# Second feed-forward product: left factors built on chip, residual and weight sums added by DMA

## Chip, cores and metric

The kernel runs on 1 core of one Trainium2 chip, in fp32 accuracy. The metric is the device time of one execution in microseconds (us).

## What is computed

One encoder layer on 512 tokens of width 2048: a branch of gated linear recurrence (mLSTM) and a branch of differential attention, mixed by gates, then a feed-forward block of width 5632. What the change touches is the end of it:

```
x = x + (g_m * branch_m + g_a * branch_a) @ w_out[l]
h2 = _rmsnorm(x, norm2_w[l])
gate, up = jnp.split(h2 @ w_ffn_in[l], 2, axis=-1)
x = x + (jax.nn.silu(gate) * up) @ w_ffn_out[l]
...
return _rmsnorm(x, final_norm_w)
```

## The kernel before

Every product is made of 128x128 by 128x512 matmuls. To keep fp32 accuracy each factor is split into a high part (a cast on ScalarE, line 151) and a low part (the difference on VectorE, line 152), and three matmuls stand for one (`mm3`).

The earlier products (aqk, av, mv, mqk, mo, ga, gm, ba, bm) are plain. The last three, wo (w_out), fi (w_ffn_in) and fo (w_ffn_out), go through `seven`: a block product of 2 by 2 blocks made with seven products instead of eight. A group g is 512 rows of the inner dimension. For it the weight comes as four blocks, 11, 12, 21 and 22, each a raw tile of 128x1024 fp32 (0.524 MB). Loads a, b, c bring 11, 12, 22, and loads d, e, f bring 21, 12, 22 once more. A chunk has three stages: Q1, Q6, Q5 for every group, then Q2, Q7, Q3 for every group, then Q4 for every group. Each is a *piece*: one split right factor and 12 matmuls. The sums of weights are made on VectorE: T2 = (b + a) + c for Q6 (lines 306 and 308), e + f for Q7 (line 314), T2 + d for Q4 (line 320). Three pairs of PSUM banks (a, b, c) take the results; `post` runs when a stage's last group is done.

wo has 2 chunks of 4 groups, fi 11 (fi0 to fi10) of 4 groups. fo takes its 11 groups in lots of 4, 4 and 3, with 2 chunks for each lot: fo0_0, fo0_1, fo1_0, fo1_1, fo2_0, fo2_1.

The left factors are made by `make_forms`: from the four transposed blocks X11, X12, X21, X22 come seven forms (X11, S1, S2, S3, X12, S4, X22), each split, 14 half tiles of 128x512 fp32 (0.262 MB). For fi they are made from x1 (transposed by `x1_turn`) and stay on chip. For fo, fi's `post` makes them as soon as a chunk is gated (`turned`) and stores all 14 to DRAM on SyncE's queue (line 685); `lot_forms` loads them again, 56 for a lot of four, on ScalarE's queue (line 733), called when Q5 of the chunk before is done.

`added` does the residual: at Q1 it loads eight tiles of the residual (x for wo, x1d for fo) on ScalarE's queue (line 591), adds the results to them on VectorE and GpSimd (lines 593 to 609), and `final` stores them to x1d or, in the last lot, normalizes and writes the output.

The order is the program's, with three helpers. `take` makes pieces two ahead (AHEAD), `load` issues raw loads on SyncE's queue up to two sources past the piece that is made, into 5 raw buffers; `later` puts a step after so many nanoseconds of matmuls. High and low parts have 3 buffers each. The framework adds the semaphores and may order the instructions of an engine by expected readiness.

Of the kernel before, what the change touches and what calls it, by code (L numbers as in the profile page):

```python
# [12 lines left out]
F32 = mybir.dt.float32  # L13
F32R = mybir.dt.float32r
# [102 lines left out]
def build(ctx, tc, a, out):  # L117
# [7 lines left out]
    tpool = ctx.enter_context(tc.tile_pool(name="tpool", bufs=41))  # L125
# [168 lines left out]

    FORMS = ("X11", "S2", "S1", "X12", "S3", "S4", "X22")

    def seven(name, src, ng, forms, post):

        first = len(pieces)

        def raw(g, half, lot, n):
            return source(f"{name}_{n}{g}", src(g, half, lot))

        def t2_make(r11, r12, r22, t2, g):
            def make(nm):
                V.tensor_tensor(raws[r12], raws[r12], raws[r11], ALU.add)
# [20 lines left out]
        t2 = {}  # L327
        for g in range(ng):
            r = [raw(g, 0, 0, "a"), raw(g, 0, 1, "b"), raw(g, 1, 1, "c")]
            piece(f"{name}_q1{g}", r[0], held(lambda r=r: raws[r[0]]))  # L330
            piece(f"{name}_q6{g}", r[2], t2_make(*r, t2, g))
            piece(f"{name}_q5{g}", r[2], held(lambda r=r: raws[r[1]]))
        for g in range(ng):
            r = [raw(g, 1, 0, "d"), raw(g, 0, 1, "e"), raw(g, 1, 1, "f")]
            piece(f"{name}_q2{g}", r[0], t4_make(r[0], t2, g))
            piece(f"{name}_q7{g}", r[2], t3_make(r[1], r[2]))
            piece(f"{name}_q3{g}", r[2], held(lambda r=r: raws[r[2]]))
        for g in range(ng):
# [819 lines left out]
```

## Time and profile before

| | us |
|---|---|
| median of 3 runs | 2817.01 (2814.28 to 2817.61) |
| profiled execution | 2818.14 |
| its span | 2816.4 |
| TensorE busy | 2688.4 (95%) |
| VectorE busy | 1914.6 (68%) |
| ScalarE busy | 1173.3 (42%) |
| GpSimd busy | 206.8 (7%) |
| DMA | 477.03 MB, 169 GB/s on the mean |

The products before w_out fill the span up to 1210.9 us, wo runs to 1391.1, fi to 2297.2, fo to 2803.6. "Granted clock" is the share of TensorE's full clock that was granted in a stretch; "DMA share" is the mean busy share of the core's 16 DMA engines. Matmuls overlap in the pipeline, so the distance from one start to the next is what a matmul costs, and not its own duration.

### The profile page before, as it was taken

How to read it: one execution, taken by the hardware profiler on the slowest of the kernel's cores; microseconds unless marked ns; L12 is line 12 of the kernel's file. 1: busy time of each engine (PE TensorE's matmuls, PEld its weight loads, DVE VectorE, ACT ScalarE, POOL GpSimd, SP SyncE). 2: the span in 40 equal slices, each digit the busy share in tenths (PEclk: the TensorE clock that was granted, in tenths of full speed). 3: DMA queues.
4: the chain of work that ended last, by engine and by line, in shares of the span. 5: the costliest groups of instructions: out<-in, count | busy, mean ns of one | idle time of the engine just before them, and what ended most of it. 6: DMA issues, size and time to landing. Idle time of an engine off the chain costs nothing.

```text
span 2816.4 us, 33558 instructions
## 1 busy us (share of the span) xinstructions
PE 2688.4 (95%) x12736; PEld 2227.1 (79%) x12736; DVE 1914.6 (68%) x2385; ACT 1173.3 (42%) x1659; POOL 206.8 (7%) x208
## 2 busy tenths in 40 slices
PE   8999999999999999989999999999999798789897
PEld 6888888888998888877777788888877677577676
DVE  6677775333444433677988888888888777467677
ACT  5444443222444432334745555544445343233343
POOL 3000000000000000011000000000000001110111
PEclk9999999999999999999999999999999999899999
DMA  6433232333222232455446665655566876867845
GB/s 204 125 93 91 77 109 102 112 112 120 90 85 93 80 110 97 140 170 199 160 157 213 224 209 206 205 191 183 201 215 219 282 258 229 301 237 243 285 167 177
DMA packets 168850, 477.03 MB, mean 169 GB/s; under 512 B 20376, under 2 KB 20936, under 8 KB 168688
## 3 DMA queue, kind: packets, MB, share of 16 engines
q1 hardware_dynamic: 125280, 392.89, 40.8%
q10 hardware_dynamic: 35616, 63.46, 6.8%
q0 software_dynamic: 7792, 18.54, 2.5%
q8 instruction: 100, 1.64, 0.2%
q14 instruction: 62, 0.51, 0.1%
HBM read 402.96 MB, written 61.36 MB: 165 GB/s over the span
## 4 chain that ended last, share of the span: by engine, by line
PE 70%; DVE 12%; DMA 11%; issue 3%; ACT 2%; POOL 1%; ACTq 1%; SPq 0%; DVEq 0%; POOLq 0%
PE fi_b L147 9%; PE ga_b L147 6%; PE gm_b L147 6%; PE aqk_b L147 5%; PE fi_c L147 5%; DVE wlo_fi_q L152 4%; PE fi_a L147 4%; PE fo_b L147 3%; PE mqk_b L147 3%; PE mo_b L147 3%; PE bm_b L147 3%; PE ba_b L147 3%; PE fo_a L147 3%; PE mv_p L147 3%; DMA raw_fi_f<-in_w_ffi 3%
## 5 line engine op out<-in xcount | busy, mean ns | idle before, releaser
L151 ACT CAST whi_fi_q<-fi_q_t 128x1024 fp32r<-128x1024 f32 x88 | 92.5, 1052 | 150.2 <-DVE fi_q_t L308 70.1
L147 PE MATMUL fo_c<-whi_fo_q,fs_S 128*128 128x512 f32 x352 | 119.6, 401 | 13.9 <-ACT whi_fo_q L151 13.4
L147 PE MATMUL fo_a<-whi_fo_q,fs_X 128*128 128x512 f32 x352 | 123.4, 412 | 2.7 <-ACT whi_fo_q L151 2.6
L147 PE MATMUL fo_b<-whi_fo_q,fs_S 128*128 128x512 f32 x352 | 120.0, 401 | 2.1 <-DVE fo_x L593 1.6
L152 DVE TENSOR_TENSOR wlo_fi_q<-fi_q_t,whi_fi_q 128x1024 fp32r<-128x1024 f32 x88 | 106.6, 1221 | 10.2 <-ACT whi_fi_q L151 9.0
L147 PE MATMUL aqk_b<-xh,whi_aqk 128*128 128x512 f32 x256 | 101.3, 398 | 7.7 <-ACT whi_aqk L151 7.7
L147 PE MATMUL aqk_b<-xl,whi_aqk 128*128 128x512 f32 x256 | 101.5, 397 | 3.9 <-DVE xl L483 3.9
L702 POOL TENSOR_TENSOR fv<-fv,fv 128x512 f32<-128x512 f32 x22 | 44.3, 2033 | 794.5 <-ACT fv L701 794.5
L147 PE MATMUL aqk_b<-xh,wlo_aqk 128*128 128x512 f32 x256 | 100.8, 394 | 0.3 <-DVE wlo_aqk L152 0.3
L147 PE MATMUL ga_b<-xh,whi_ga 128*128 128x512 f32 x256 | 99.9, 390 | 0.0
L147 PE MATMUL gm_b<-xh,whi_gm 128*128 128x512 f32 x256 | 99.7, 389 | 0.0
L147 PE MATMUL ga_b<-xl,whi_ga 128*128 128x512 f32 x256 | 99.7, 389 | 0.0
L147 PE MATMUL ga_b<-xh,wlo_ga 128*128 128x512 f32 x256 | 99.7, 389 | 0.0
L147 PE MATMUL gm_b<-xl,whi_gm 128*128 128x512 f32 x256 | 99.6, 389 | 0.0
L147 PE MATMUL gm_b<-xh,wlo_gm 128*128 128x512 f32 x256 | 99.6, 389 | 0.0
L147 PE MATMUL fo_a<-wlo_fo_q,fs_X 128*128 128x512 f32 x176 | 74.4, 423 | 24.9 <-DVE wlo_fo_q L152 24.9
L152 DVE TENSOR_TENSOR wlo_gm<-raw_gm,whi_gm 128x1024 fp32r<-128x1024 f32 x32 | 39.2, 1225 | 84.4 <-ACT whi_gm L151 84.4
L314 DVE TENSOR_TENSOR raw_fi_e<-raw_fi_e,raw_fi_f 128x1024 f32<-128x1024 f32 x44 | 56.0, 1272 | 57.6 <-DMA raw_fi_f<-in_w_ffi 57.6
L147 PEld LDWEIGHTS fo_c<-whi_fo_q,fs_S 128*128 128x128 f32 x352 | 68.6, 195 | 29.4 <-ACT whi_fo_q L151 14.2
L147 PEld LDWEIGHTS fo_a<-whi_fo_q,fs_X 128*128 128x128 f32 x352 | 70.3, 201 | 18.4 <-ACT whi_fo_q L151 3.5
L147 PEld LDWEIGHTS fo_b<-whi_fo_q,fs_S 128*128 128x128 f32 x352 | 68.4, 194 | 18.6 <-DVE fo_x L593 2.8
L147 PE MATMUL fi_c<-whi_fi_q,h_S4h 128*128 128x512 f32 x176 | 69.5, 396 | 13.0 <-ACT whi_fi_q L151 13.0
(494 smaller groups left out, 8500.9 us busy)
## 6 DMA issues: line engine op xcount, KB each, us to landing
raw_fi_a<-in_w_ffi SPq DMA_DIRECT2D x44, 512.0 KB, 4.6
raw_fi_b<-in_w_ffi SPq DMA_DIRECT2D x44, 512.0 KB, 3.5
raw_fi_c<-in_w_ffi SPq DMA_DIRECT2D x44, 512.0 KB, 4.7
raw_fi_d<-in_w_ffi SPq DMA_DIRECT2D x44, 512.0 KB, 4.9
raw_fi_e<-in_w_ffi SPq DMA_DIRECT2D x44, 512.0 KB, 4.5
raw_fi_f<-in_w_ffi SPq DMA_DIRECT2D x44, 512.0 KB, 4.5
fs_S<-fg_S ACTq DMA_DIRECT2D x88, 256.0 KB, 4.7
fs_X<-fg_X ACTq DMA_DIRECT2D x66, 256.0 KB, 4.9
```

What stands on the lines that cost most here:

```text
L147: T.matmul(dst, lhs[l], rhs[r], start=first and i == 0, stop=last and i == 2, skip_group_check=skip)
L151: A.copy(hi, src)
L152: V.tensor_tensor(lo, src, hi.bitcast(F32), ALU.subtract)
L314: V.tensor_tensor(raws[r12], raws[r12], raws[r22], ALU.add)
L702: G.tensor_tensor(v5[i], v5[i], v1[i], ALU.subtract)
```

## The change

- Raw buffers go from 5 to 6, loads run three sources ahead instead of two, and the work tiles go from 41 to 39.
- A source may have a second part (`plus`): GpSimd's queue adds it to the raw tile by an accumulating DMA once the plain load has landed. So b arrives as 11 + 12 and e as 12 + 22, and the sums of lines 306 and 314 are gone. Weight blocks 11 and 22 are read once more for that.
- The pieces go Q1, Q5, Q6, then Q2, Q3, Q7 (the last group Q7, Q3, Q2), then Q4.
- fi keeps only the four transposed blocks of each chunk (`turned`, half a chunk at a time, after Q2 and after Q4), stored on ScalarE's queue. fo loads three of them and then all four on GpSimd's queue (`loaded`) and builds the seven forms again on ScalarE and VectorE, one step behind each piece (`ahead`, `work`), from the start of Q2 in the chunk before. The left factors of h2 are made in the same way, for the first two column blocks by way of DRAM.
- The residual: Q1's result is copied into three tiles by ScalarE, the other results are added by VectorE alone. In fo0 and fo1 the tile is added to x1d by an accumulating DMA; in wo and fo2 the residual is added to the tile by one before the tile's square is taken.
- The last scaling is split: three of the four tiles of a row are multiplied by the norm's weight early, and the last factor goes to ScalarE for two tiles and VectorE for two.

```diff
-            raw = wpool.tile([P, src.shape[-1]], F32, tag="raw", name=f"raw_{name}", bufs=5)
+            raw = wpool.tile([P, src.shape[-1]], F32, tag="raw", name=f"raw_{name}", bufs=6)
             nc.sync.dma_start(raw, src)
+            if plus is not None:
+                G.dma_start(raw, plus, accum_op=ALU.add)
...
-            load(need + 2)
+            load(need + 3)
...
+    def work(must=False):
+        if behind:
+            ready_, fn = behind[0]
+            while must and not ready_():
+                tasks.pop(0)[1]()
+            if ready_():
+                behind.pop(0)
+                fn()
...
-                V.tensor_tensor(raws[r12], raws[r12], raws[r11], ALU.add)
...
-                V.tensor_tensor(raws[r12], raws[r12], raws[r22], ALU.add)
...
+        for g in order:
+            r = [raw(g, 0, 0, "a"), raw(g, 0, 1, "b", (0, 0)), raw(g, 1, 1, "c")]
+            add("Q1", g, r[0], held(lambda r=r: raws[r[0]]))
+            add("Q5", g, r[1], held(lambda r=r: raws[r[1]]))
+            add("Q6", g, r[2], t2_make(r[1], r[2], g))
+        for g in order:
+            if g != order[-1]:
+                r = [raw(g, 1, 0, "d"), raw(g, 1, 1, "f"), raw(g, 0, 1, "e", (1, 1))]
...
+                w = take(it)
+                while LEFT[q_] not in forms(g):
+                    work(True)
...
+                if g == order[-1]:
+                    post(q_, bank)
+                work()
...
+    def loaded(name, g, out, src):
+
+        def load1():
+            out["ld1"] = X = {k: half(f"{name}_1{k}") for k in ("X11", "X21", "X22")}
+            for k, t in X.items():
+                G.dma_start(t, src[k].rearrange("p (k c) -> p k c", k=2))
...
+        def s4():
+            X = out["ld2"]
+            V.tensor_tensor(X["X12"], X["X12"], X["X22"], ALU.subtract)
+            V.tensor_tensor(X["X12"], X["X12"], X["X21"], ALU.subtract)
+            factor(name, g, 10, out, "S4", X["X12"])
...
+        return (load1, [x11, s1, s2]), (load2, [x12, s3, s4, x22])
+
+    def ahead(steps):
+
+        for n, (ld, fns) in enumerate(steps):
+            if n == 0 and ld:
+                ld()
+            nxt = steps[n + 1][0] if n + 1 < len(steps) else None
+
+            def head(fn=fns[0], nxt=nxt):
+                if nxt:
+                    nxt()
+                fn()
+            behind.extend([(lambda: True, fn) for fn in [head] + fns[1:]])
...
+        def fetch(q, i):
+            G.dma_start(x[q, i], src(*place(q, i)), accum_op=ALU.add)
+
+        def end(q, i):
+            t, c = place(q, i)
+            if final:
+                final(t, c, x[q, i])
+            else:
+                G.dma_start(x1d[t][c], x[q, i], accum_op=ALU.add)
...
                 if q_ == "Q1":
...
+                    for q, sc in ((22, -1.0), (12, -1.0), (21, 1.0)):
+                        A.activation(tile_(q, i), a_[i], AF.Copy, scale=sc)
+                    if final:
+                        fetch(21, i)
...
+                elif q_ == "Q7":
+                    V.tensor_tensor(x[22, i], x[22, i], b_[i], ALU.subtract)
+                    if final:
+                        fetch(22, i)
+                    end(22, i)
...
+            if q_ == "Q2":
+                later(5000, lambda: turned(f"fg{j}", u2, 0, X, 0, fgd[j]))
+            elif q_ == "Q4":
+                later(8000, lambda: turned(f"fg{j}", v5, 0, X, 1, fgd[j]))
...
+        both = [loaded(f"fs{g}", i, fgf[g], fgd[g]) for i, g in enumerate(LOTS[m])]
+        ahead([b[0] for b in both] + [b[1] for b in both])
...
+        def final(t, c, x):
+            j = t_(f"x2j{t}_{c}")
+            A.activation(j, x, AF.Square, accum_out=ss3p[:, t * 4 + c:t * 4 + c + 1])
```

## Rows read from the trace of the kernel before

**Rows 1.** The page's line of TensorE: busy us (share of the span) and instructions.
```profile
PE 2688.4 (95%) x12736; PEld 2227.1 (79%) x12736; DVE 1914.6 (68%) x2385; ACT 1173.3 (42%) x1659; POOL 206.8 (7%) x208
```

**Rows 2.** Stretches: bm; then wo0, wo1, fi1, fi10, fo0_0 to fo2_1, the tail.
```profile
core 0: us, PE busy (x) PEld busy (x) DVE busy (x) ACT busy (x) POOL busy (x), PEclk, DMA share, GB/s
1124.00:1211.00 87.00, 87.00 (x386) 72.03 (x385) 62.25 (x96) 29.85 (x40) 6.43 (x12) 1.00 0.42 139
...
1210.90:1297.50 86.60, 79.49 (x337) 64.27 (x336) 69.00 (x74) 37.81 (x49) 9.42 (x6) 0.94 0.57 186
1297.50:1391.10 93.60, 87.36 (x394) 69.69 (x392) 75.51 (x84) 54.10 (x89) 9.46 (x6) 0.96 0.52 175
...
1471.90:1552.30 80.40, 78.67 (x353) 64.39 (x352) 69.68 (x72) 39.92 (x51) 3.00 (x2) 1.00 0.60 205
...
2193.50:2297.20 103.70, 84.67 (x353) 67.19 (x352) 70.11 (x72) 39.70 (x51) 3.12 (x2) 0.90 0.84 297
2297.20:2386.20 89.00, 81.29 (x353) 65.81 (x352) 70.62 (x73) 37.61 (x47) 11.32 (x6) 0.94 0.68 233
2386.20:2492.20 106.00, 86.36 (x338) 67.44 (x337) 59.45 (x56) 30.19 (x30) 9.44 (x6) 0.90 0.85 289
2492.20:2576.30 84.10, 79.54 (x337) 64.69 (x336) 61.67 (x58) 30.48 (x30) 9.44 (x6) 0.96 0.63 211
2576.30:2672.80 96.50, 82.81 (x337) 65.59 (x336) 60.45 (x57) 30.31 (x30) 9.46 (x6) 0.95 0.86 288
2672.80:2739.50 66.70, 61.07 (x253) 49.10 (x253) 47.72 (x46) 26.68 (x35) 9.43 (x6) 0.92 0.53 180
2739.50:2803.60 64.10, 60.26 (x253) 48.01 (x251) 46.73 (x51) 25.91 (x37) 12.86 (x12) 0.97 0.46 154
2803.60:2816.40 12.80, 0.16 (x1) 0.00 (x0) 7.93 (x16) 1.33 (x4) 1.10 (x2) 0.60 0.65 238
```

**Rows 3.** Chain that ended last, bm's matmuls: start us, us, engine, tile, count.
```profile
1124.04 87.04 PE bm_b L147 x384
```

**Rows 4.** Stretch of one transposition in fi, its instructions alone (PE, PEld, ACT).
```profile
1481.20:1484.20 3.00, 2.24 (x16) 1.77 (x16) 1.95 (x7) 1.00 0.59 220
```

**Rows 5.** Timelines of ScalarE and TensorE in fo0_1: start us, us [idle before <-releaser].
```profile
2444.92 1.04 ACT L151 CAST whi_fo_q<-raw_fo_f 128x1024 fp32r<-128x1024 f32 x1 [20.95 <-DMA fs_X<-fg_X]
...
2446.01 1.22 PE L147 MATMUL fo_c<-whi_fo_q,fs_S 128*128 128x512 f32 x2 [9.21 <-ACT whi_fo_q L151]
```

**Rows 6.** The stretch of that gap, columns as in rows 2.
```profile
2430.00:2447.00 17.00, 7.45 (x22) 5.35 (x22) 6.65 (x6) 2.08 (x3) 3.63 (x2) 0.72 0.99 348
```

**Rows 7.** Waits, whole span and wo: us in total, times, longest us.
```profile
SPq L198 <- DVE wlo_fi_q L152: 501.4, 187, 7.2
...
ACT wo_v L586 <- DMA wo_x<-in_x: 12.3, 2, 9.1
```

**Rows 8.** Groups of instructions: busy us, mean ns of one | idle before.
```profile
L152 DVE TENSOR_TENSOR wlo_fi_q<-fi_q_t,whi_fi_q 128x1024 fp32r<-128x1024 f32 x80 | 96.8, 1221 | 8.5 <-ACT whi_fi_q L151 7.2
...
L306 DVE TENSOR_TENSOR raw_fi_b<-raw_fi_b,raw_fi_a 128x1024 f32<-128x1024 f32 x40 | 48.8, 1221 | 37.4 <-DMA raw_fi_b<-in_w_ffi 37.4
...
L152 DVE TENSOR_TENSOR fg_S1l<-fg_S,fg_S1h 128x512 fp32r<-128x512 f32 x9 | 6.2, 683 | 0.0
...
L586 ACT COPY fo_v<-fo_a 128x512 f32<-128x512 f32 x12 | 7.1, 588 | 28.2 <-DMA fo_x<-x1d 16.0 <-PE fo_a L147 4.9 <-issue 4.0
```

**Rows 9.** DMA queues (q1 SyncE's, q0 GpSimd's), and an issue: KB, us to landing.
```profile
q1 hardware_dynamic: 125280, 392.89, 40.8%
...
q0 software_dynamic: 7792, 18.54, 2.5%
...
fo_x<-x1d ACTq DMA_DIRECT2D x48, 256.0 KB, 5.5
```

**Rows 10.** GpSimd's timeline in bm and in fo2_1: DMA issues and additions.
```profile
1161.16 1.07 POOL L524 DMA_DIRECT2D mixa<-mixa_d  x2 [2.53 <-DVE mix_X L530]
...
2765.47 2.31 POOL L596 TENSOR_TENSOR fo_x<-fo_x,fo_v 128x512 f32<-128x512 f32 x1 [1.50 <-DMA fo_x<-x1d]
2767.73 2.23 POOL L771 DMA_DIRECT2D fnw<-in_fnw  x4
2769.97 2.53 POOL L594 TENSOR_TENSOR fo_x<-fo_x,fo_v 128x512 f32<-128x512 f32 x2
```

More of the change, by code (lines that the diff above doesn't have):

```diff
@@ L338, in seven, with add @@
-        for g in range(ng):
-            piece(f"{name}_q4{g}", 0, held(lambda g=g: t2[g]))
+        def add(q_, g, need, make):
+            piece(f"{name}_{q_}{g}", need, make)
+            seq.append((q_, g))
+        for g in order:
[3 more added lines that the diff above has]
+            add("Q6", g, r[2], t2_make(r[1], r[2], g))
@@ L642, in wo_chunk @@
-        inner = added(f"wo{n}", n, lambda t, c: a["x"][t][:, c * 512:(c + 1) * 512], final)
-        def post(q_, bank):
-            inner(q_, bank)
-            if n == 1 and q_ == "Q5":
-                for c in env.pop("turns"):
-                    x1_turn(c)
-        seven(f"wo{n}", lambda g, h_, l: a["w_out"][n, g, h_, l], 4, lambda g: mixf[g], post)
+            A.activation(j, x, AF.Square, accum_out=ss2p[:, t * 4 + c:t * 4 + c + 1])
+            x1[t, c] = x
+            i = t // 2
+            if (2 * i, c) in x1 and (2 * i + 1, c) in x1:
+                pair = [x1.pop((2 * i + k, c)) for k in range(2)]
+                later(4000, lambda: turned(f"h2{c}", pair, 0, h2X[c], i,
+                                           h2d[c] if n == 0 else None,
+                                           lambda kk: n2w[:, c * 4 + kk:c * 4 + kk + 1]))
@@ new lines, in start @@
+        def start(q_):
+            if n == 1 and q_ == "Q2":
+                for g in range(4):
+                    h2f[g] = {}
+                p0, p1 = (loaded(f"h2{c}", c, h2f[c], h2d[c]) for c in range(2))
+                p2, p3 = (kept(f"h2{c}", c, h2f[c], h2X[c]) for c in (2, 3))
+                ahead([p0[0], p1[0], p0[1]])
+                for c, p in ((3, p3), (2, p2)):
+                    when(lambda c=c: len(h2X[c]) >= 4, p[0])
+                when(lambda: True, [p1[1][0]] + p1[1][1])
+                when(lambda: True, p3[1] + p2[1])
@@ L651, in rstd2 @@
+        seven(f"wo{n}", lambda g, h_, l: a["w_out"][n, g, h_, l], range(4), lambda g: mixf[g],
+              added(f"wo{n}", n, lambda t, c: a["x"][t][:, c * 512:(c + 1) * 512], final), start)
     def rstd2():
@@ L756, in norm, with start @@
             pow_rstd(r, ss, D, 1)
[L757 to L766 removed]
+            for k, (c, x) in enumerate(mine):
+                if k == 3:
+                    V.scalar_tensor_tensor(x, x, r, env["fnw"][c], ALU.mult, ALU.mult)
+                elif k == 2:
+                    V.tensor_scalar(x, x, r, None, ALU.mult)
+                else:
+                    A.activation(x, x, AF.Copy, scale=r)
+                (nc.sync if k > 1 else nc.scalar).dma_start(
+                    out[t][:, c * 512:(c + 1) * 512], x)
+        def start(q_):
+            if q_ == "Q2" and n == 1 and not last:
                 lot_forms(m + 1)
[L768 removed]
+            if q_ == "Q1" and n == 0 and last:
                 env["fnw"] = [t_(f"fnw{c}") for c in range(4)]
@@ L773, in fo_chunk @@
         lot = LOTS[m]
[L774 to L775 removed]
+        seven(f"fo{m}_{n}", lambda g, h_, l: a["w_ffo"][n, g, h_, l], lot, lambda g: fgf[g],
+              added(f"fo{m}_{n}", n, *((lambda t, c: x1d[t][c], final) if last else ())), start)
     fin = {}
```

347 lines of the change are left out of this document (167 added, 180 removed).

## Prediction

> **What bounds the kernel now.** I read the page first: TensorE is busy 95% of the span [rows 1], so a gain must come from its gaps. The second view is the table of stretches, one for each chunk of the two last products and w_out [rows 2]. Its first row is a stretch of bm, an ordinary projection: TensorE 87.00 of 87.00 us, with VectorE at 62.25 us (72%) and DMA at 0.42. The chain of waits prices a full matmul there: 384 in 87.04 us, 226.7 ns each [rows 3]. That makes a floor: a chunk of 4 groups is 28 pieces of 12 matmuls, 336 x 0.2267 = 76.2 us; one of 3 groups is 252, 57.1 us. Sixteen transposes cost 2.24 us [rows 4].
>
> Against that floor [rows 2]: the wo chunks take 86.6 and 93.6 us, together 27.8 above it, of which the 64 transposes of h2 explain up to 9.0; fi0 to fi9 run from 1391.1 to 2193.5, 802.4 us, 40.4 above ten floors, half of it nine sets of transposes (20.2); fi10 is 27.5 above; the four chunks fo0_0 to fo1_1 take 375.6, 70.8 above; fo2_0 and fo2_1 together 16.6 above. About 150 us of real gaps, most of them in fi10 and fo. The granted clock says the same: 1.00 in fi1, 0.90 to 0.96 in fi10 and the four fo chunks, so these stretches hold gaps and slowed matmuls.
>
> Who causes them? The timelines show one gap whole [rows 5]: ScalarE sits 20.95 us until a DMA that loads left factors (fs_X) has landed, then casts weights; 1.1 us later TensorE resumes after 9.21 us idle. In that stretch DMA is at 0.99 and 348 GB/s [rows 6]: 56 loads of 0.262 MB for a lot of four groups stand in ScalarE's queue, ahead of the casts, and fill the DMA engines. I take 348/0.99, about 350 GB/s, as what they can move. The same queue waits up to 9.1 us for the residual in wo [rows 7]. In fi the gap is another: SyncE's queue waits 501 us in all for wlo to free a raw buffer [rows 7], with VectorE at 69.68 of 80.40 us [rows 2]; VectorE frees late, so loads start late, but TensorE loses only 1.8 to 2 us a chunk.
>
> **What the change removes.** (a) One sum in q6 and one in q7 for each group: 2 x 1.221 us of VectorE [rows 8], 9.8 us a chunk of 4, 74 groups in all, 181 us. In fi also 7 low parts and 4 sums of 0.683 us (7.5 us) leave, so VectorE falls from 69.7 to about 69.7 - 9.8 - 7.5 + 1.4 (v5 now made there) = 54 us of 79, 68%, under the 72% that bm sustains with no gap. (b) 14 stores a fi chunk, on SyncE between the weight loads, become 4 on ScalarE. (c) 56 loads for a lot of four become 28, on GpSimd's queue, spread one group at a time, so no cast stands behind them. (d) Residual loads leave ScalarE; fo0 and fo1 don't load x1 at all. (e) All additions on GpSimd go, so nothing there delays the accumulating DMAs that stand in its queue; its issue of one DMA takes 0.54 us (1.07 for two) [rows 10], 4.3 us for 8.
>
> **What it adds.** In fo each lot is rebuilt: 7 casts on ScalarE, and on VectorE 7 low parts and 5 sums, 12 x 0.683 = 8.2 us a group. They run one step behind each piece. At the handover fi10 to fo0_0 the sixteen pieces from Q2 on last 43.5 us; VectorE has in them 16 x 1.221 for low parts, 4 x 1.221 for sums, 27 form operations (18.4) and 8 gating ones (5.6): 48.4 us. The next twelve pieces (32.6 us) hold 12 low parts, 4 sums, 21 form operations and 6 gating ones, 38. A deficit of 10 us less the lead of two pieces (5.4): I take 6 for fi10. From fo to fo gating is missing and the deficit is about 6 in all; I take 4 for each of those chunks, which covers the bank changes too. ScalarE's copies at Q1 go from 2 to 6, 6 x 0.588 [rows 8] = 3.5 us, and bank a is overwritten two pieces (5.4 us) later: hidden, at 0; without that lead each would cost up to 3.5 us in 8 chunks. Transposes come in two batches of 8, same cost. In fi I leave 0.7 us a chunk, in wo 3, in fo2 5: there the square on ScalarE waits until an accumulating fetch of the residual, issued only after VectorE's last operation on the tile, has landed, and today's plain fetch lands after 5.5 us [rows 9].
>
> What GpSimd's queue holds: a weight sum there waits until SyncE's load has landed, and behind it wait the factor loads and the residual. A raw buffer turns over in 6 x 2.72 = 16.3 us instead of 13.6, and b or e needs two landings, about 10 us, and then its split, 2.3 us. It fits, with some 4 us to spare; if not, pieces of Q5 and Q7 come late.
>
> **The unknown price** is an accumulating DMA; none is in this trace. It can't be below one plain transfer of its bytes. A plain byte on GpSimd's queue takes 1.3 times SyncE's share: 18.54 MB in 2.5% against 392.89 in 40.8% [rows 9]. Read and write of the old contents in a second pass of that kind gives 2 x 1.3 = 2.6. With c for the price in plain transfers, c = 1 to 2.6. I take 2, the bytes read twice at the ordinary price; it is nearest to q1's row, by which both the load and the write-back run at full rate. The Trainium skill (DMA: Bandwidth & Descriptors, SDMA does more than copy) says of the adding unit that it reduces two streams; by that two reads are due and c is 2 rather than 1, worth 22 us of the sum below. No run here shows it yet.
>
> In MB a chunk moves (raw tile 0.524, half tile 0.262): wo 18.1 + 5.8c, fi 13.6 + 4.2c, fi10 17.3 + 4.2c, fo0 and fo1 16.3 + 6.3c (24 weights, 8 weight sums, 8 sums into x1, 14 factors), fo2 12.5 + 4.7c. At 350 GB/s with c = 2 that is 85, 63, 73, 82.5 and 63 us. On TensorE's side: wo 76.2 + 4.5 + 3 = 83.7; fi 76.2 + 2.2 + 0.7 = 79.1; fi10 84.4; fo 76.2 + 4 = 80.2; fo2 57.1 + 5 = 62.1. The larger counts, and 1 us more where both are near (8 chunks; my choice).
>
> **The sum**: 1210.9 before wo0 (a sixth raw buffer and two work tiles fewer act there too; TensorE has no room for more than a few us either way, I take 0) + 2 x 85 + 10 x 79.1 + 84.4 + 4 x 82.5 + 2 x 63 + 8 + 11 (the tail, 12.8 now [rows 2], with the last eight scalings of VectorE split over two engines) = 2731 us of span. The profiled run takes 2818.1 with a span of 2816.4 and lies 1.1 above the median of 2817.0, so 1.7 is added and 1.1 taken off: 2732, 85 us or 3.0% under the median. By place: wo 8, fi0 to fi9 11, fi10 19, fo0 and fo1 42, fo2 3, tail 2.
>
> **The rivals.** A, accumulating is nearly free: c = 1, each chunk on TensorE's side, 2710; with the waits that I left at nothing too, about 2665. For: fi has DMA at 0.60 [rows 2], so the transfers have room. Against: the engine must read the old contents. B, a wait takes the place of the one removed: in the wo and fo2 chunks the four fetches stand in ScalarE's and VectorE's order one behind the other, 4 x 5.5 - 5.4 = 16.6 us a chunk, four chunks, 66 less the 16 already counted: 2782. Against it: the instructions don't stand in program order; in [rows 10] the loads of fnw, which come before L594 to L596 in the program text, run behind L596, so the order follows expected readiness, and such a wait can be put later. C, c is 2.6: fo0 and fo1 are DMA's at 93 us, wo at 95, fo2 at 71: 2801. D, **slower**: an accumulating transfer costs more than about 2.7 plain ones. Then the DMA engines bound fo first, then wo and fo2: at c = 3 100, 101 and 76 us, 2853 in all; at c = 4 fi turns as well (87 us) and the sum is 3077. For: the change puts 78 MB of such weight reads where DMA is already at 0.46 to 0.86 [rows 2]; nothing in the trace excludes it. Against: it would need over twice the price of the dearest plain byte. The Trainium skill (SBUF — State Buffer, Summary: rules for kernel authors) also speaks against the move: it says that a DMA issued by GpSimd should not be hidden under VectorE, since descriptor writing starves in VectorE's two-port modes. The trace doesn't show it for this kernel's operations: the two loads at 1161.16 were issued in 1.07 us [rows 10] with VectorE at its sums; I add nothing for it. E, the change does what it says, but what leaves one stage is given back in another, c near 2.7: within 0.2%.
>
> **How the numbers follow.** Forecast (c about 1.5 to 2.3, 2716 to 2762) 0.50; A 0.20; B and C with their middle ground (2762 to 2811) 0.12; E 0.04; D 0.14. The forecast is the likeliest one's 2732. The range runs from 2688, inside A, to 2805, past C; it leaves out D and E, a little of A and the last of C, 2 in 10. About 0.2% (5.6 us) is what a measurement of this kernel can tell from no change. Faster 0.82, within 0.2% 0.04, slower 0.14.
>
> **What would show it.** Right: fi chunks at about 79 us with VectorE near 54; no cast waits for a factor load beyond a few us; fi10 near 84; fo0 and fo1 80 to 85 with a granted clock of 0.97 and up; DMA above 0.9 there; fourteen fewer DMAs on SyncE's queue in each fi chunk. c is read from the accumulating DMAs' share for their MB. Wrong: DMA at 0.99 through fo with chunks over 90 us (C or D); gaps of 5 us and more behind Q7 and Q3 in wo and fo2 (B); fi over 80.4; a gap at the handover of much more than 6 us.

## The result, and the profile after

The changed kernel takes **2917.1 us** (median of 4, 2908.9 to 2925.8), the kernel before 2817.1 beside it: a ratio of 1.036 [1.033, 1.039]. The forecast was 2732, 85 us faster; the change made the kernel 100 us slower, so the forecast has the wrong sign. Its profiled execution took 2908.9 us with a span of 2907.0; the span before was 2816.4.

First the page: the busy times of the engines, which answer [rows 1], and the two weight queues, which answer [rows 9] (MB, share of 16 engines).

```profile
PE 2709.4 (93%) x12736; PEld 2253.7 (78%) x12736; DVE 1729.1 (59%) x2268; ACT 1186.0 (41%) x1641; POOL 324.8 (11%) x457
...
q1 hardware_dynamic: 96192, 339.92, 33.9%
q0 software_dynamic: 46368, 140.98, 23.1%
```

VectorE lost 186 us of work and GpSimd's queue took over 122 MB, as the change says. TensorE's share fell from 95% to 93%: it has more gaps. The table of stretches says where; its rows are wo0, wo1, fi0, fi1 to fi9, fi10, fo0_0 to fo1_1, and the two chunks of fo2 (columns as in [rows 2]).

```profile
1214.30:1315.40 101.10, 85.00 (x361) 67.70 (x360) 58.07 (x67) 44.34 (x65) 16.64 (x22) 0.93 0.81 226
1315.40:1421.10 105.70, 86.72 (x370) 69.86 (x369) 64.84 (x72) 49.96 (x79) 23.15 (x34) 0.92 0.80 230
1421.10:1503.20 82.10, 78.57 (x354) 64.54 (x353) 65.95 (x79) 43.20 (x57) 10.62 (x14) 1.00 0.78 224
1503.20:2288.60 785.40, 727.85 (x3169) 595.22 (x3168) 481.35 (x487) 315.60 (x342) 61.85 (x72) 0.96 0.73 205
2288.60:2380.30 91.70, 82.66 (x354) 67.48 (x353) 65.13 (x76) 42.47 (x52) 17.86 (x28) 0.94 0.80 242
2380.30:2749.40 369.10, 328.46 (x1353) 264.12 (x1352) 254.58 (x288) 164.08 (x204) 85.35 (x119) 0.94 0.85 242
2749.40:2894.80 145.40, 125.54 (x505) 99.72 (x504) 91.42 (x105) 62.09 (x90) 27.08 (x35) 0.92 0.74 195
```

Against [rows 2]: wo loses 14.5 and 12.1 us, fi0 to fi9 65.1 (867.5 for 802.4), fo2 14.6; fi10 gains 12.0, fo0_0 to fo1_1 6.5; 3.4 are lost ahead of wo0 and 0.6 won in the tail. That is the 90.6 us between the two spans. In fi the mean chunk is 87.3 us, the granted clock 0.96 (it was 1.00) and the DMA share only 0.73, so neither VectorE (53.5 us a chunk) nor the DMA engines are full. Something waits.

The waits by engine name it (us in total, times, longest), TensorE's first, then VectorE's and ScalarE's; they answer [rows 7].

```profile
PE fi_a L147 <- DVE wlo_fi_Q L152: 59.6, 12, 6.4
PE fo_b L147 <- DVE wlo_fo_Q L152: 30.5, 14, 3.8
PE fo_c L147 <- DVE wlo_fo_Q L152: 18.9, 7, 4.9
PE h_T L731 <- DMA wo_x<-in_x: 18.0, 4, 8.6
...
DVE fi_Q_t L330 <- DMA raw_fi_d<-in_w_ffi: 129.3, 31, 8.4
DVE fi_Q_t L323 <- DMA raw_fi_b<-in_w_ffi: 53.7, 27, 4.6
...
ACT x2j L857 <- DMA fo_x<-x1d: 15.4, 5, 11.3
```

TensorE waits in fi for a low part (wlo) ahead of bank a, 12 times, about once a chunk and 5 us each. VectorE, which makes it, waits for a DMA: for d (L330 adds d to T2) and for b (L323 makes T2 from b and c). The timelines of fi5 show how the two belong together. SyncE's queue first (start us, us), from the loads of the last group's a, b and c and the first group's d:

```profile
1851.19 0.33 SPq L198 DMA_DIRECT2D raw_fi_a<-in_w_ffi  x1
1857.19 0.33 SPq L198 DMA_DIRECT2D raw_fi_b<-in_w_ffi  x1
1861.00 0.33 SPq L198 DMA_DIRECT2D raw_fi_c<-in_w_ffi  x1
1862.13 0.33 SPq L198 DMA_DIRECT2D raw_fi_d<-in_w_ffi  x1
```

GpSimd issues the adding transfer into that b when its load has landed:

```profile
1861.70 0.85 POOL L200 DMA_DIRECT2D raw_fi_b<-in_w_ffi  x1 [8.28 <-DMA raw_fi_b<-in_w_ffi]
```

VectorE in the same stretch, with idle time and releaser in brackets:

```profile
1862.03 1.22 DVE L152 TENSOR_TENSOR wlo_fi_Q<-fi_Q_t,whi_fi_Q 128x1024 fp32r<-128x1024 f32 x1
1870.77 1.23 DVE L330 TENSOR_TENSOR fi_Q_t<-fi_Q_t,raw_fi_d 128x1024 f32<-128x1024 f32 x1 [7.53 <-DMA raw_fi_d<-in_w_ffi]
1871.92 1.22 DVE L323 TENSOR_TENSOR fi_Q_t<-raw_fi_b,raw_fi_c 128x1024 f32<-128x1024 f32 x1
1873.05 1.22 DVE L152 TENSOR_TENSOR wlo_fi_Q<-raw_fi_a,whi_fi_Q 128x1024 fp32r<-128x1024 f32 x1
```

And TensorE:

```profile
1868.59 0.39 PE L147 MATMUL fi_a<-whi_fi_Q,h_X11h 128*128 128x512 f32 x1
1874.33 0.79 PE L147 MATMUL fi_a<-wlo_fi_Q,h_X11h 128*128 128x512 f32 x1 [5.35 <-DVE wlo_fi_Q L152]
```

The low part of the **third** group's a (1873.05) doesn't lack its data: the matmul at 1868.59 already reads the high part of the same a. But ahead of it on VectorE stand the first addition of d and the **fourth** group's T2, whose operands are still in flight, and VectorE doesn't go past them: it idles 7.53 us, TensorE 5.35, and the next matmuls run longer (0.79 and 0.63 us instead of 0.39). This isn't the order of the program's text, where the fourth group's T2 comes behind five low parts that it here precedes (the third group's three and the fourth group's first two). The experiments below test whether this is the cause or only the place.

For them one measure is used throughout, worked out from the starts of TensorE's matmuls: the time from a product's first matmul to the next product's, mean over fi1 to fi9. An undisturbed product takes 2.72 us (12 x 0.2267). In the changed kernel 24 of the 28 products of a chunk take 2.72 to 2.91, two carry transposes (3.6 each), and two carry the loss: the third group's Q1, 10.43, and the third group's Q3, 3.94.

### The profile page after: what moved, and what is told of

Read it like the earlier page. It is cut to its first block, busy times and chain, and to the rows that moved or that the text cites. A ratio compares the mean times of both kernels' runs of the same rounds, so it can differ in the third digit from the quotient of the medians.

```text
span 2907.0 us, 33614 instructions
## 1 busy us (share of the span) xinstructions
PE 2709.4 (93%) x12736; PEld 2253.7 (78%) x12736; DVE 1729.1 (59%) x2268; ACT 1186.0 (41%) x1641; POOL 324.8 (11%) x457
## 3 DMA queue, kind: packets, MB, share of 16 engines
q1 hardware_dynamic: 96192, 339.92, 33.9%
q0 software_dynamic: 46368, 140.98, 23.1%
## 4 chain that ended last, share of the span: by engine, by line
PE 57%; DMA 24%; DVE 9%; issue 7%; ACT 2%; POOL 1%; SPq 0%; ACTq 0%; POOLq 0%; DVEq 0%
PE ga_b L147 6%; PE gm_b L147 6%; DMA raw_fi_b<-in_w_ffi 6%; PE fi_b L147 5%; PE aqk_b L147 5%; PE fi_c L147 4%; PE fi_a L147 4%; DMA raw_fi_d<-in_w_ffi 4%; PE mqk_b L147 3%; PE mo_b L147 3%; PE ba_b L147 3%; DMA raw_fo_b<-in_w_ffo 3%; DVE wlo_fi_Q L152 3%; PE mv_p L147 3%; PE av_p L147 2%
## 5 line engine op out<-in xcount | busy, mean ns | idle before, releaser
L151 ACT CAST whi_fi_Q<-fi_Q_t 128x1024 fp32r<-128x1024 f32 x88 | 92.4, 1051 | 112.6 <-PE fi_b L147 94.8
L330 DVE TENSOR_TENSOR fi_Q_t<-fi_Q_t,raw_fi_d 128x1024 f32<-128x1024 f32 x44 | 53.9, 1224 | 129.3 <-DMA raw_fi_d<-in_w_ffi 129.3
L147 PE MATMUL fi_a<-wlo_fi_Q,h_X11h 128*128 128x512 f32 x176 | 78.7, 447 | 55.7 <-DVE wlo_fi_Q L152 55.7
L152 DVE TENSOR_TENSOR wlo_fi_Q<-fi_Q_t,whi_fi_Q 128x1024 fp32r<-128x1024 f32 x88 | 106.5, 1220 | 20.4 <-ACT whi_fi_Q L151 20.4
L151 ACT CAST whi_fi_Q<-raw_fi_a 128x1024 fp32r<-128x1024 f32 x44 | 46.3, 1052 | 122.2 <-PE fi_a L147 85.2
L323 DVE TENSOR_TENSOR fi_Q_t<-raw_fi_b,raw_fi_c 128x1024 f32<-128x1024 f32 x44 | 53.9, 1225 | 63.5 <-DMA raw_fi_b<-in_w_ffi 53.7
L147 PEld LDWEIGHTS fi_a<-wlo_fi_Q,h_X11h 128*128 128x128 f32 x176 | 38.1, 216 | 68.1 <-DVE wlo_fi_Q L152 60.3
L200 POOL DMA_DIRECT2D raw_fi_e<-in_w_ffi x44 | 37.9, 861 | 437.3 <-DMA raw_fi_e<-in_w_ffi 369.6
L151 ACT CAST whi_fi_Q<-raw_fi_e 128x1024 fp32r<-128x1024 f32 x44 | 46.3, 1053 | 98.6 <-DMA raw_fi_e<-in_w_ffi 57.1
L152 DVE TENSOR_TENSOR wlo_fi_Q<-raw_fi_d,whi_fi_Q 128x1024 fp32r<-128x1024 f32 x44 | 53.8, 1224 | 46.8 <-ACT whi_fi_Q L151 46.8
L151 ACT CAST whi_ga<-raw_ga 128x1024 fp32r<-128x1024 f32 x32 | 33.7, 1053 | 115.1 <-PE ga_b L147 62.4
```

The lines of the kernel that those rows point to most:

```text
L147: T.matmul(dst, lhs[l], rhs[r], start=first and i == 0, stop=last and i == 2, skip_group_check=skip)
L151: A.copy(hi, src)
L152: V.tensor_tensor(lo, src, hi.bitcast(F32), ALU.subtract)
L200: G.dma_start(raw, plus, accum_op=ALU.add)
L323: V.tensor_tensor(t2[g], raws[r12], raws[r22], ALU.add)
```

## The experiments

Ratios are to the kernel before on the same chip, with 95% intervals.

**The weight sums: the second transfer, and the adding.** e1_vsum makes both sums (b's is shown, e's is alike) on VectorE again, with one load each; all other parts of the change stay.

```
-  r = [raw(g, 0, 0, "a"), raw(g, 0, 1, "b", (0, 0)), raw(g, 1, 1, "c")]
+  r = [raw(g, 0, 0, "a"), raw(g, 0, 1, "b"), raw(g, 1, 1, "c")]
+  V.tensor_tensor(raws[r12], raws[r12], raws[r11], ALU.add)
```

> The changed kernel with the sums 11+12 and 12+22 made on VectorE again (two sums of 1.22 us a group); the second loads of those blocks and their accumulating DMAs are gone, all else stays. If the accumulating weight sums cause the loss in fi (fi1 to fi9 87 us a chunk against 80), fi falls to 79 to 81 us, fo by some us a chunk, and the total to about 2840 us; the 26 us lost in wo stay, since they come from the residual. If the factors built on chip or their DMAs on GpSimd's queue cause it, fi stays at 86 to 88 and the total above 2900.

**2753.2 us, 0.9775 [0.9760, 0.9789]**: this beats the kernel before by 64 us. The sums by DMA cost 164 us; the rest of the change earns 64. The stretch fi1 to fi9, and fo0_0 to fo1_1:

```profile
1470.60:2180.00 709.40, 706.11 (x3170) 580.89 (x3170) 561.55 (x560) 316.13 (x342) 0.60 (x1) 1.00 0.51 174
2262.70:2617.80 355.10, 324.21 (x1354) 259.84 (x1353) 288.95 (x319) 166.78 (x207) 55.37 (x83) 0.96 0.67 203
```

fi takes 78.8 us a chunk with VectorE at 62.4: more work on VectorE than in the changed kernel, and less time. fi came as expected; wo, which was expected to keep its loss, fell from 206.8 to 177.3 us.

e2_plain keeps every instruction in its place and takes the adding out of the second transfer; the result then lacks the weight sums.

```
-  G.dma_start(raw, plus, accum_op=ALU.add)
+  G.dma_start(raw, plus)
```

> The changed kernel with the second DMA into the raw tile as a plain one that overwrites it: the same bytes, queue and chain of two landings, but nothing is added (the weight sums are left out of the result). If the price of adding in the DMA engines is the cause (share 0.73 in fi, about 1.8 plain transfers each), the share in fi falls to about 0.63, fi to 80 to 82 us and the total to about 2850. If the chain of two loads into one buffer is what costs, fi keeps most of its stall (84 to 87 us) and the total stays above 2890.

**2789.3 us, 0.9902 [0.9882, 0.9921]**. So the second transfer costs 36 us over e1, and adding, with the same order, bytes and queue, another 128. fi takes 80.8 us a chunk at a DMA share of 0.66, as the first case had it, though the total is 61 us below that case. The wait stands where it stood, only shorter: the third group's Q1 takes 5.41 us instead of 10.43, with b complete 10.8 us after its load is issued instead of 13.8 (medians over fi). The GpSimd queue of e2 and the two landings of its b, to set beside those of the changed kernel (23.1%; 4.3 and 7.7 us):

```profile
q0 software_dynamic: 46368, 140.98, 16.9%
...
raw_fi_b<-in_w_ffi SPq DMA_DIRECT2D x44, 512.0 KB, 4.2
...
raw_fi_b<-in_w_ffi POOLq DMA_DIRECT2D x44, 512.0 KB, 6.1
```

This gives **c**. In e1 that queue has 63.38 MB and 9.2% of 2755.5 us, 253.5 us of all sixteen engines; in e2 16.9% of 2787.7, 471.1; in the changed kernel 23.1% of 2907.0, 671.5. The same 77.6 MB cost 217.6 us plain and 418.0 adding: c = 1.92.

**More buffers, fewer buffers.** The first theory behind these figures was a matter of supply: two landings hold a buffer so long that six are too few.

e4_raw7 has seven raw buffers, loads four ahead, and two work tiles fewer.

```
-  raw = wpool.tile([P, src.shape[-1]], F32, tag="raw", name=f"raw_{name}", bufs=6)
+  raw = wpool.tile([P, src.shape[-1]], F32, tag="raw", name=f"raw_{name}", bufs=7)
-  load(need + 3)
+  load(need + 4)
```

> The changed kernel with seven raw buffers and loads four sources ahead, and 37 work tiles for 39. If buffers that are held for two landings (some 14 us) are what bounds it, a seventh (2.7 us more of lead) takes half of the stall or more: fi 80 to 84 us, total 2850 to 2880. If the order on VectorE is the cause, d still comes late for a sum that stands too early: the stall falls by at most 2.7 us a chunk, fi 84 to 87, total 2890 to 2917.

2857.7 us, 1.0136 [1.0112, 1.0160]; fi 82.1 us a chunk, both in the range of that theory. But the place of the loss moved: the third group's Q1 is at 2.72 us, and the chunk now loses at the first group's Q5 (3.95) and Q6 (5.38). In fi5 a T2 waits 4.87 us for c there, ahead of the low part of the first group's b. So the seventh buffer also changed where VectorE waits, and e4 can't tell supply from order.

e8_before_plus puts the adding transfers alone into the kernel before (five buffers, loads two ahead; the text below says three), for b as shown and for e:

```
-  r = [raw(g, 0, 0, "a"), raw(g, 0, 1, "b"), raw(g, 1, 1, "c")]
+  r = [raw(g, 0, 0, "a"), raw(g, 0, 1, "b", (0, 0)), raw(g, 1, 1, "c")]
-  V.tensor_tensor(raws[r12], raws[r12], raws[r11], ALU.add)
```

> The kernel before (2817 us) with one thing added: the sums of b and e are made by a second, adding transfer instead of by VectorE, with its five raw buffers and loads three ahead as before, and its own order of products, store and reload of the factors, and residual. Theory (landings times buffers): a summed buffer holds its place for some 16 us, the six of a group some 125 to 131 us as in the changed kernel, with five buffers 100 to 105 us a chunk in fi (80 before), in all 3000 to 3080 us. Rival 1 (adding loads the DMA engines, whatever the buffers): 84 to 88 us in fi, 2870 to 2920 us. Rival 2 (VectorE was the bound in this kernel, and is freed of 9.8 us a chunk): 2790 to 2815 us.

3089.8 us, 1.0979 [1.0942, 1.1016]: 273 us for this part alone, just past what the theory named in all, but not where it named it. fi takes 826.1/9 = 91.8 us and not 100 to 105; fo0_0 to fo1_1 take 115.9 each (93.9 before):

```profile
1519.40:2345.50 826.10, 747.45 (x3169) 599.00 (x3169) 540.56 (x568) 354.90 (x459) 97.66 (x90) 0.96 0.76 223
2459.10:2922.70 463.60, 347.54 (x1361) 272.38 (x1360) 221.03 (x209) 127.13 (x137) 59.59 (x56) 0.89 0.80 246
```

That a buffer more helps, e4 shows (59 us); e8 differs from the changed kernel in more than its buffers. Full DMA engines don't show in either stretch: 0.76 and 0.80.

**Where the summed buffer stands among the loads.** e7_first loads b (shown) and e first in their groups; same bytes, same work.

```
-  r = [raw(g, 0, 0, "a"), raw(g, 0, 1, "b", (0, 0)), raw(g, 1, 1, "c")]
+  r = [raw(g, 0, 1, "b", (0, 0)), raw(g, 0, 0, "a"), raw(g, 1, 1, "c")]
```

> The changed kernel (2917 us) with only the order of the loads altered: b is loaded ahead of a and c, and e ahead of its two neighbours, so that the two landings of a summed buffer begin one load (2.7 us) earlier. Same bytes, same adding, same buffers, same order of work. Theory (the two landings and the split of a summed buffer fill the 16.3 us in which six buffers turn over, so TensorE is left with no lead): part of the 2.7 us comes back as lead, 2 to 5 us in each fi chunk, in all 2860 to 2900 us. But b then holds its buffer longer and is released after a, whose buffer the next b wants; if that takes back what is gained, 2910 to 2930. Rival (the adding transfers slow all others by their load on the DMA engines): 2910 to 2920, with fi at 87 us as in the changed kernel.

**2794.5 us, 0.9920 [0.9904, 0.9937]**, 123 us under the changed kernel and 66 under the best that the theory gave it; fi 80.1. One place in the queue, 2.7 us, couldn't explain that. e12_b_last moves b one place back instead (a, c, b).

> The changed kernel (2917 us) with only the loads of a group's first half in another order: a, c, b, where it has a, b, c; e stays where it is. Same bytes and work. With b and e first in their groups fi took 79 to 84 us a chunk, against 86 to 88 us in the changed kernel. Theory (a summed buffer must begin its two landings early, and each place that it is moved back costs lead, in the same measure as each place forward gained it): b moved back by one of the four places that the run with b and e first moved it and e forward makes the sum of the six holds some 4 us longer, 90 us a chunk in fi, in all 2945 to 2990 us. Rival (what gained there was the place of e alone, or the order in which GpSimd issues): 2905 to 2930 us.

2897.2 us, 1.0275 [1.0242, 1.0307]: **faster** than the changed kernel by 20 us. The theory that each place earlier gains, and each later costs, fell here. e13_e_first and e14_b_first move e alone and b alone:

> The changed kernel (2917 us) with e loaded first in its group of three, b where it was. On VectorE the last group's sum for Q6 then stands ahead of the first addition of d. If e's place is what gained 123 us with both moved: 2795 to 2830 us. If b's place is: 2880 to 2915. If both are needed alike: 2840 to 2870.

> The changed kernel (2917 us) with b loaded first in its group of three, e where it was. On VectorE the last group's sum for Q6 then stands ahead of the first addition of d here too. If e's place is what gained 123 us with both moved: 2880 to 2915 us. If b's place is: 2795 to 2830. If both are needed alike: 2840 to 2870.

e13: 2883.6 us, 1.0248 [1.0226, 1.0270]. e14: 2815.5 us, 1.0007 [0.9994, 1.0021]. It is b's place, 102 of the 123 us. e16_last_e_first moves e ahead of f in the last group alone:

> The changed kernel (2917 us) with one load moved by one place in each chunk: in the last group, e ahead of f, whose product uses e first. The order on VectorE stays that of the changed kernel. If what costs time is that the last two summed loads stand two apart and that the last e is wanted first (two pairs of landings within 5.4 us of loads): 2870 to 2890 us, most of it in fi and fo at their second half. If the seam between the two halves and the place of b and of the other e cost it: 2905 to 2920 us.

2926.3 us, 1.0393 [1.0364, 1.0422]: nothing gained, that rival is out.

**The order on VectorE.** What tells e12 and e14 from e13 and e16 is what stands on VectorE ahead of the third group's a. In e12 the low part of that a comes ahead of the fourth group's T2 (behind the addition of d alone). In e14 and e7 T2 still stands ahead of it (and d in e14), but b is issued ahead of a hole in SyncE's queue, 6.0 us in which no buffer is free; in the changed kernel it stands behind it (a at 1851.19, b at 1857.19). The same loads in fi5 of e7:

```profile
1815.76 0.33 SPq L198 DMA_DIRECT2D raw_fi_b<-in_w_ffi  x1
1821.76 0.33 SPq L198 DMA_DIRECT2D raw_fi_a<-in_w_ffi  x1
1822.89 0.33 SPq L198 DMA_DIRECT2D raw_fi_c<-in_w_ffi  x1
```

So b gains 6 us, not 2.7. That is an early b. The other way is a late reader: four kernels leave the loads as they are and only hold additions back, with an operand that a later instruction delivers (1.0 in a tile `pin`). e3_pin holds the first addition of d until the last group's T2 is split:

```
-  V.tensor_tensor(t2[g], t2[g], raws[r21], ALU.add)
+  V.scalar_tensor_tensor(t2[g], raws[r21], pin["last"], t2[g], ALU.mult, ALU.add)
```

> The changed kernel with the sum T2 + d held back on VectorE until the low part of the last group's Q6 is made (a factor of 1 that is written then, one small operation a chunk more). In the changed kernel this sum stands before the last group's T2 on VectorE and waits there up to 7.5 us for d. If that order is the cause, the wait falls on nothing that TensorE needs: fi1 to fi9 come to 79 to 81 us, the total to about 2850. If loads are late because six raw buffers don't cover two landings, the wait moves to the next operation that needs d or b: fi 84 to 87 us, total above 2890.

2892.9 us, 1.0275 [1.0246, 1.0304]: 24 us, and fi at 85.9 us a chunk, the second case: the wait moved to the next operation. T2 still stands ahead, and it now waits for b (7.16 us in fi5). e17_pin_t holds T2 instead, until the low part of the group before's a is done, and leaves d ahead; e18_pin_both holds both:

```
-  V.tensor_tensor(t2[g], raws[r12], raws[r22], ALU.add)
+  V.scalar_tensor_tensor(t2[g], raws[r12], pin[order[p]], raws[r22], ALU.mult, ALU.add)
```

> The changed kernel (2917 us) with each group's sum for Q6 (b + c) held back on VectorE until the low part of the group before's a is done; the first addition of d stays ahead of the third group's a. Loads, bytes and buffers as in the changed kernel. Theory (VectorE, in order, stands at an operand that two landings make late, and the low part behind it is what TensorE waits for): the wait moves from b to d, which is loaded two places later and lands once; 82 to 86 us a chunk in fi, 2870 to 2910 us. Rival (b is simply late, whatever stands behind it): 86 to 89 us, 2910 to 2935.

> The run before with the first addition of d held back too, until the last group's sum is split, so that nothing that waits for a load stands ahead of the third group's a. Theory (order on VectorE): the wait at the third group's first product goes, 79 to 82 us a chunk in fi as with b loaded first, in all 2800 to 2850 us. Rival (b is late whatever the order; held-back additions hold b, c and d longer in their buffers): the wait comes back at the third group's last product or at the second half's first, 85 to 89 us a chunk, 2880 to 2930 us.

e17: 2880.0 us, 1.0212 [1.0177, 1.0248], the theory's case. e18: 2855.0 us, 1.0136 [1.0106, 1.0167], a little past the theory's range and far from the rival's. The third group's Q1 is at 2.72 in e18, but its Q5 at 6.14. VectorE shows why; the low part of a runs now (1844.09), and T2 waits for b ahead of the low part of the third group's **b**:

```profile
1844.09 1.23 DVE L152 TENSOR_TENSOR wlo_fi_Q<-raw_fi_a,whi_fi_Q 128x1024 fp32r<-128x1024 f32 x1 [1.72 <-ACT whi_fi_Q L151]
...
1850.42 1.28 DVE L325 SCALAR_TENSOR_TENSOR fi_Q_t<-raw_fi_b,pin,raw_fi_c 128x1024 f32<-128x1024 f32 x1 [4.92 <-DMA raw_fi_b<-in_w_ffi]
1851.62 1.22 DVE L152 TENSOR_TENSOR wlo_fi_Q<-raw_fi_b,whi_fi_Q 128x1024 fp32r<-128x1024 f32 x1
```

e19_pin_group holds each T2 until the group before's own T2 is split (`pin` from there).

> The changed kernel (2917 us) with each group's sum for Q6 held back on VectorE until the low part of the group before's own Q6 is done, and the first addition of d until the last group's is; loads, bytes and buffers as in the changed kernel. Theory (order on VectorE): no product of the third group has an unlanded operand ahead of its low part, and fi takes 79 to 80.5 us a chunk as with b loaded first, in all 2805 to 2840 us. Rival (b is late in itself, or the sums held back keep b and c longer in their buffers): 82.5 us or more a chunk, 2850 us or more.

**2816.0 us, 1.0003 [0.9983, 1.0023]**, 101 us under the changed kernel with its loads, bytes and buffers unchanged. T2 (1843.48) finds its operand half a microsecond late and stands in nobody's way:

```profile
1841.50 1.23 DVE L152 TENSOR_TENSOR wlo_fi_Q<-fi_Q_t,whi_fi_Q 128x1024 fp32r<-128x1024 f32 x1 [1.49 <-ACT whi_fi_Q L151]
1842.76 0.15 DVE L330 TENSOR_SCALAR pin<-wlo_fi_Q 128x1 f32<-128x1 f32 x1
1843.48 1.28 DVE L325 SCALAR_TENSOR_TENSOR fi_Q_t<-raw_fi_b,pin,raw_fi_c 128x1024 f32<-128x1024 f32 x1 [0.56 <-DMA raw_fi_b<-in_w_ffi]
```

```profile
1504.10:2220.90 716.80, 708.01 (x3169) 584.01 (x3168) 491.70 (x523) 315.37 (x342) 62.22 (x72) 1.00 0.80 225
```

fi takes 79.6 us a chunk, the clock is 1.00 again, and the DMA share **rose** to 0.80: the transfers had room all along. The products that differ, in us (mean over fi1 to fi9, worked out as above; g3 is the third group; "ahead" is what VectorE has ahead of that group's a: the addition of d, the fourth group's T2):

```
                    ahead            g3 Q1   g3 Q5   g3 Q3   chunk
changed kernel      d, T2            10.43    2.91    3.94   87.3
e3_pin              T2                9.78    2.85    3.35   85.9
e17_pin_t           d                 8.91    2.93    3.46   85.3
e12_b_last          d                 4.81    3.98    3.67   84.1
e18_pin_both        nothing           2.72    6.14    3.70   82.5
e19_pin_group       nothing           2.72    2.72    4.11   79.7
e13_e_first         T2                9.69    2.90    2.72   86.2
e14_b_first         T2, d, b early    3.37    2.72    3.82   79.8
e7_first            T2, b early       2.96    4.54    2.72   80.1
```

(e12 loses another 1.2 us at three products of the first two groups.) The small loss at Q3 goes with e's place: of these kernels only e13 and e7, which load e first, are without it.

**Residual fetches, and the best of both.** e6_vsum_early is e1 with the residual's fetches of two quadrants issued one addition earlier: x22's behind that of Q5 instead of Q7, x12's behind that of Q6 instead of Q3, eleven products sooner.

```
    elif q_ == "Q5":
        V.tensor_tensor(x[22, i], x[22, i], c_[i], ALU.add)
+       if final: fetch(22, i)
```

> The kernel with the weight sums back on VectorE (2753 us), and beside it the residual's adding fetches of the second and first quadrant of x1 and x2 issued one product earlier, as soon as their own last VectorE addition but one is done. In the run with VectorE's sums alone the transposes of h2 still waited for the fetch (four waits of about 8 us in the two wo chunks, and the like in fo2). Theory (the landing of an adding fetch lies on the path at the ends of wo and fo2): the two wo chunks lose 10 to 15 us and the two fo2 chunks 3 to 6, in all 2733 to 2742 us. Rival (the waits stand beside the weights of the next chunk, which would be late anyway): within 4 us of 2753.

2750.2 us, 0.9772 [0.9754, 0.9791], the rival's case. e9_vsum_early_raw7 adds a seventh buffer:

> The kernel of VectorE's sums and earlier fetches with seven raw buffers instead of six, loads four ahead, 37 work tiles instead of 39. In fi its buffers do not hold it up (78.8 us a chunk at a floor of 76.2, clock 1.00), so theory expects nothing there: 2725 to 2742 us, a few us from fo, where the handover between chunks still waits for VectorE's splits. Rival (the buffers bind there too): fi falls by 2 us a chunk, 2712 to 2722 us.

2749.5 us, 0.9760 [0.9745, 0.9774], the fastest median, 67 us under the kernel before beside it; not to be told from e6. Its fi got 1.4 us a chunk slower and its fo faster, neither as expected. The same two additions on top of e7, in two steps:

> The changed kernel with both cures: b and e loaded first in their groups (2794 us alone), and seven raw buffers, loads four ahead, 37 work tiles (2858 us alone). Theory (landings times buffers; with six buffers and this order the holds come to 120 us, 80 us a chunk, still above the floor of 76.2): fi 77 to 79 us a chunk as with VectorE's sums, fewer waits in wo and fo, in all 2740 to 2765 us. Rival (the adding transfers' load on the DMA engines sets what is left): 2780 to 2795 us.

> The run with both cures, and the residual's adding fetches of the first and second quadrant issued one product earlier. With VectorE's sums this gave 3 us at most. Theory (the landing of these fetches is on the path at the ends of wo and fo2 only where the adding transfers of the weights stand in GpSimd's queue ahead of them): 5 to 15 us under the run with both cures. Rival (the weights of the next chunk are as late as the fetch): within 4 us of it.

e10: 2792.3 us, 0.9906 [0.9879, 0.9932]: fi fell to 78.9 a chunk (710.3 for fi1 to fi9, DMA 0.82, clock 1.00), as theory had it, but wo took 202.5 us instead of e7's 192.7, so nothing is left of it: the total is the rival's, but the rival's reason, the load on the DMA engines, doesn't fit that fi. e11: 2786.4 us, 0.9884 [0.9860, 0.9907], 6 us better by the medians, with intervals that overlap. In the two profiled executions, 12 us apart, wo falls from 202.5 to 190.5 and fo2 from 143.4 to 136.2, and fi0 gives 5 back.

## Why the prediction was wrong, step by step

**The step that failed** stands under "What GpSimd's queue holds": two landings, about 10 us, and a split fit into the 16.3 us in which a buffer turns over, "with some 4 us to spare; if not, pieces of Q5 and Q7 come late". The landings alone take 4.3 + 7.7 = 12.0 us, and in the changed kernel the summed b is first read 14.0 us after its load is issued (median over 36 groups of fi, worked out from the trace). But the size is the smaller fault: e14 and e19 live with the same landings at 80 us a chunk. The step asked only whether b would come late for its **own** piece. It didn't ask which instruction on VectorE waits for b (the T2 of L323), where that stands in VectorE's order, and what is queued behind it: the low part of a piece that is wanted a whole group sooner. The loss is at the third group's Q1, neither a Q5 nor a Q7. e19 shows it: order alone returns 7.6 us a chunk of fi. In the profiled executions that is 69 us in fi and 20 in fo0 and fo1; wo and fo2 get nothing from it.

That early place of T2 was harmless only as long as its operands had landed. e1 has the same place: in fi5 the fourth group's T2 and an addition of d stand ahead of the third group's a, and wait 0.21 and 1.24 us.

```profile
1798.78 1.23 DVE L323 TENSOR_TENSOR fi_Q_t<-raw_fi_b,raw_fi_c 128x1024 f32<-128x1024 f32 x1 [0.21 <-DMA raw_fi_c<-in_w_ffi]
1801.24 1.23 DVE L330 TENSOR_TENSOR fi_Q_t<-fi_Q_t,raw_fi_d 128x1024 f32<-128x1024 f32 x1 [1.24 <-DMA raw_fi_d<-in_w_ffi]
1802.39 1.22 DVE L152 TENSOR_TENSOR wlo_fi_Q<-raw_fi_a,whi_fi_Q 128x1024 fp32r<-128x1024 f32 x1
```

The prediction had seen that instructions leave the program's order, but used it only against rival B, as a way to put a wait later; here it put one earlier. What made VectorE's order so, and whether another could be had at no cost from the program's text, was not examined.

**Right: c.** Forecast 2, measured 1.92; the two ends were 1 and 2.6. A MB took 5.39 us of all sixteen engines instead of 2.80. This agrees with the Trainium skill (DMA: Bandwidth & Descriptors, SDMA does more than copy), by which the adding unit reduces two streams. The dearer plain byte on GpSimd's queue, from which the 2.6 came, doesn't show in e2: 2.80 us a MB there, 2.93 on SyncE's queue (35.7% of 2787.7 us for 339.92 MB). So **rival D** had the sign with the wrong mechanism: it needed c above 2.7 and full DMA engines, and they ran at 0.73 in fi, 0.81 in wo and 0.85 in fo0 and fo1. No rival held the cause.

**GpSimd's issue.** The prediction misread a row here: VectorE was not "at its sums" during the two issues at 1161.16, but idle for 2.20 us, until 1163.06. e2 has what that row lacked: its 88 plain issues in fi take 0.53 to 0.55 us each, and 54 of them lie almost wholly in VectorE's busy time without taking longer than the others. The Trainium skill (SBUF — State Buffer, Summary: rules for kernel authors) ties the starving of descriptor writing to VectorE's 2x and 4x modes. No run here shows in which mode VectorE ran, so that rule stays untested.

**Right, and worth nothing: VectorE at 54 us in fi** (53.5). e1 has 62.4 and is faster. VectorE's busy time didn't bind fi; the moment at which its next instruction may start did.

**fi10, 84**: 91.7 in the changed kernel, 82.7 in e1. The cost of the sums hid a step that was right.

**fo0 and fo1, 82.5 by DMA**: 92.3 on average. Here a size was wrong too. In e1 the DMA share is 0.67, so bytes don't bind, and a chunk takes 88.8: what lies between chunks costs 12.6 us above the floor of 76.2, where the working took 4. With b early it is 85.9 (e7). Of the 42 us forecast for this place e1 has 20.5, the changed kernel 6.5. Of the signs set out, chunks over 90 us came, but at a DMA share of 0.85 and not 0.99; and casts do wait for loaded factors, four times for X12, up to 9.5 us.

**wo and fo2, 296 together**: 352.2. This is **rival B's** place: transposes of h2 wait 18.0 us for the residual, the square in fo2 15.4, on landings of 8.5 to 9.7 us where 5.5 was taken from [rows 9]. Without the weight sums the two products take 302.8 (e1): the transposes still wait 8.3 us for the same fetches, the square 6.9, and e6's earlier issue gives no more than 3 us in all. With the weight sums earlier issue took 12 us off wo and 7 off fo2 (e11, one profiled execution each).

But the residual is only a part of it. TensorE's waits for split weights in wo grow as well, from 3.6 us in e1 to 16.8. And e8 has no adding fetch at all, and its wo takes 217.8 us, where the kernel before takes 180.2; its longest waits there are all for split weights:

```profile
PE wo_a L147 <- DVE wlo_wo_q L152: 23.2, 2, 11.7
PE wo_b L147 <- DVE wlo_wo_q L152: 15.4, 5, 4.8
PE wo_c L147 <- DVE wlo_wo_q L152: 8.1, 4, 3.2
```

So the weight sums by DMA can cost wo time by themselves. That they also delay the fetches in GpSimd's queue fits (9.7 us to landing in wo, 5.3 in e1), but was not isolated: e7's fetches land in 5.3 us too and its wo still takes 192.7. Of the 63 us between e19 and e1, 29 are in wo, 21 in fo2 and some 18 in fi, less 6 in fo0 and fo1; this stays open.

**By place**, what the changed kernel took over the terms of the sum (the 8 us for near cases counted apart): fi0 to fi9 76.5 us, fo0 and fo1 39, wo 37, fo2 19, fi10 7, ahead of wo0 and tail 5.

## What to carry to other kernels

When a transfer takes over an engine's addition, the result comes later, and what counts is who reads it first: find that reader in its engine's order, and price what is queued behind it and wanted sooner than the reader itself. A busy share that falls is no gain unless that engine's own work was what ended the wait; here VectorE was rid of 186 us of work and the kernel became 100 us slower. Where a buffer is filled by two transfers in series, see whether its first one can be issued ahead of a hole in the queue (here 102 us for one line), or hold its reader back behind everything that is wanted sooner (101 us). Which place in the queue is the better has to be tried: one place back gained 20 us as well (e12). Either cure alone brought back only the time of the kernel before; leaving the sums on VectorE (e1) was faster than either by 62 us.

## What the runs showed of the hardware

- An adding DMA from DRAM takes 1.92 times the engine time of a plain one on the same queue (418.0 against 217.6 us for 77.6 MB), but landed only 1.6 to 1.9 us later for 512 KB: 7.7 for 6.1 us, and 6.7 for 4.8 (b and e, the changed kernel and e2).
- GpSimd's issue of it takes 0.86 us (61.85 us for 72) instead of 0.54 (38.62 for 72, e2).
- With these transfers the DMA share in fi went up to 0.82 at 227 GB/s with TensorE at a granted clock of 1.00 (e10). A chunk took 78.9 us there, where its matmuls and transposes alone come to 78.4: a DMA share that looks high, and at most 0.5 us a chunk lost beside it.
